# Six modulation rows copied to all partitions by DMA through DRAM, in place of GpSimd's partition broadcast, in a diffusion block with a 32-expert layer

## The chip, the cores and the metric

The kernel runs on one core of a Trainium2 chip. The metric is the device time of one execution in microseconds, as the median of several executions. Names of engines in the rows: PE is TensorE's matmul side (PEld its weight loads), DVE is VectorE, ACT is ScalarE, POOL is GpSimd, SP is SyncE, which here only issues DMAs. A name with a q (SPq, ACTq) is the engine's instruction queue.

## The reference

One layer over 256 latent tokens and 256 context tokens of width 1024, all in float32. What bears on the change:

```python
mod = (silu(c) @ w_mod + b_mod)[:, None, :]
sh1, sc1, g1, sh2, sc2, g2 = split(mod, 6)          # six rows of 1024 numbers, one for all tokens
u = modulate(rmsnorm(x, norm1_g), sh1, sc1)         # h * (1 + scale) + shift
p = u @ w_in
q, k, v, a_raw, beta = gdn_inputs(p, conv_w, rows)
o, _, _ = gdn_bidir(q, k, v, a_raw, beta, a_log, dt_bias, s_f, s_b)   # chunked scan, both directions
x = x + g1 * merge_branches(p, o, gdn_norm_g, w_fourier_out, w_gdn_out, w_merge_out)
h2 = modulate(rmsnorm(x, norm2_g), sh2, sc2)
x = x + g2 * moe_ffn(h2, ...)                       # top 4 of 32 experts, 3 matrices of 1024x1024 each
return rmsnorm(x, final_norm_g)
```

merge_branches gates two branches with sigmoid(p @ columns) and maps them to width 1024 three times (w_gdn_out, w_fourier_out, w_merge_out).

## The kernel before

Tokens lie on the 128 partitions in two tiles for the last stages. So the rows g1, sh2, (1 + sc2) * norm2_g and g2, which are the same for every token, are wanted as tiles of 128 equal rows. `fill_mod` computes them as two tiles `mr` (kept in `mrow2`) whose partitions 0, 32, 64 and 96 hold four pieces of 512 numbers: `mrow2[0]` holds g1 and sh2, `mrow2[1]` holds (1 + sc2) * norm2_g and g2. The helper `spread` then makes a 128 x 512 tile of one piece. Six calls stand in the text after the loop over w_gdn_out (tiles with the tags ff, ye and bv, which other stages used before), two more (g2b) at the start of the experts:

```python
def spread(b, j, dst):
    G.partition_broadcast(dst, mrow2[b][32 * j:32 * j + 1, :])
    return dst
```

Weights of the first part arrive in pieces of 128 x 1024 (`raw`, three buffers, issued by SP in a fixed order). `wsplit` makes two rounded halves of each: `hi` is a copy by ACT (line 156) and `lo = raw - hi` by POOL or DVE (line 157); three buffers of each. A product is three matmuls, lines 164 to 166 (w_hi by u_hi, w_hi by u_lo, w_lo by u_hi), so that the matmul of line 166 is the first that needs `lo`. SP can issue the piece after the next two only when `lo` of a piece is done.

A scheduler sets each engine's order when the program is built, and each engine then runs its list strictly in order. In the stretch of interest the scan over chunks (lines 725 to 787) is interleaved with matmuls that don't depend on it. The last of these are the eight gates b0 to b7 of `fill_gates` (`gate(1, j, ...)`, psum tile `ps_pf`, output `gb`): POOL makes `lo` for b0, b2, b4 and b6, DVE for the others. After the scan come its normalization (line 825 squares on ACT, 827 on DVE, 829 `ms` on POOL, 831 on DVE, transposes 837 on PE), the eight pieces of w_gdn_out, eight pieces of w_merge_out, the router, and the experts.

The experts' weights (384 transfers of 1 MB, `we`, line 809) are issued by SP, up to 17 ahead, each into a page that a matmul must first have released. At the start of the experts POOL makes `ow` (line 1075), the two g2b tiles, `g2r` (line 1179) from them, and `biasr` (lines 981 and 984), which the matmul of line 1112 needs.

Of the kernel before, what the change touches and what calls it, by code (L numbers as in the profile page):

```python
# [10 lines left out]
F32 = mybir.dt.float32  # L11
# [86 lines left out]
def hybrid_block(es: ExitStack, tc: tile.TileContext, cst, x, c, ctx, c_ctx, w_mod, b_mod, norm1_g, norm2_g, w_in,  # L98
# [3 lines left out]
    V, A, G, PE, SP = nc.vector, nc.scalar, nc.gpsimd, nc.tensor, nc.sync  # L102
# [13 lines left out]
    def P(tag):  # L116
        return ps.tile([128, 512], F32, name="ps_" + tag, tag=tag, bufs=_nb[tag])

    def T(tag):
        return tmp.tile([128, 512], F32, name=tag, tag=tag, bufs=_tb[tag])  # L120

    def sm(name, *shape):
        return cp.tile([128, *shape], F32, name=name)
# [7 lines left out]
    def load(src, name, tag="pg"):  # L131
        t_ = page(name, tag=tag)
        n = src.shape[1]
        SP.dma_start(out=t_.rearrange("p (a b) -> p a b", a=n), in_=src)
        return t_.rearrange("p (a b) -> p a b", a=n)
# [67 lines left out]
    for hc in range(2):  # L203
        wm.append([page("wm").rearrange("p (k w n) -> p k w n", k=2, w=2) for k in range(4)])
        for k in range(8):
            SP.dma_start(out=wm[hc][k // 2][:, k % 2],
                         in_=w_mod[0, k * 128:(k + 1) * 128, 0:2048].rearrange("p (w n) -> p w n", w=2)[:, :, 512 * hc:512 * hc + 512])
# [65 lines left out]


    mrow2 = []

    def fill_mod():
        for b in range(2):
            o = 2048 + 2048 * b
            mr = T("mr") if b == 0 else sm("mr1", 512)  # L280
            V.memset(mr, 0.0)
            G.dma_start(out=mr[0:128:32, :], in_=b_mod[0, o:o + 2048].rearrange("(j n) -> j n", j=4))
            pm = P("pf")
            for k in range(8):
                wq = load(w_mod[0, k * 128:(k + 1) * 128, o:o + 2048].rearrange("p (a n) -> p a n", a=4), "wmb")
                for j in range(4):
                    mm(pm[32 * j:32 * j + 32, :], scT[:, k, :], wq[:, j, :], start=(k == 0), stop=(k == 7))
                yield
            if b == 1:
                nr = T("rr")  # L290
                V.memset(nr, 1.0)
                G.dma_start(out=nr[0:64:32, :], in_=norm2_g.rearrange("o (j n) -> (o j) n", j=2))
                V.tensor_scalar_add(mr[0:64], mr[0:64], 1.0)
            V.tensor_tensor(out=mr, in0=pm, in1=mr, op=ALU.add)
            if b == 1:
                V.tensor_tensor(out=mr, in0=mr, in1=nr, op=ALU.mult)
            mrow2.append(mr)

    def take(gen, n=1):
        for _ in range(n):  # L300
            next(gen, 0)

    fm = fill_mod()
    pb = P("pf")
    for k in range(8):
# [16 lines left out]
        j = 32 * (k % 4)  # L322
# [134 lines left out]
    for t2 in range(2):  # L457
        pv = pkk[t2].rearrange("p (m n) -> p m n", n=64)
        kd = T("bv").rearrange("p (m n) -> p m n", n=64)
        q = slice(8 * t2, 8 * t2 + 8)  # L460
# [247 lines left out]
    for s in range(2):  # L708
# [3 lines left out]
        for n in range(4):  # L712
# [8 lines left out]
            for g in range(2):  # L721
                gs = slice(512 * g, 512 * g + 512)
                bv = T("bv")
# [22 lines left out]
                if not last:  # L746
                    ye = T("ye")
# [99 lines left out]
    for j in range(8):  # L847
# [7 lines left out]
        V.tensor_tensor(out=mg[:, 0:256], in0=mg[:, 0:256], in1=gab[0][:, j, :], op=ALU.add)  # L855
        A.copy(mT[0][:, j, :], mg[:, 0:256])
        V.tensor_tensor(out=mT[1][:, j, :], in0=mg[:, 0:256], in1=mT[0][:, j, :].bitcast(F32), op=ALU.subtract)
    def spread(b, j, dst):
        G.partition_broadcast(dst, mrow2[b][32 * j:32 * j + 1, :])
        return dst  # L860

    g1b, sh2b, a2b = [[spread(b, 2 * q + j, T(tag)) for j in range(2)] for b, q, tag in ((0, 0, "ff"), (0, 1, "ye"), (1, 0, "bv"))]
    x_pg = load(x[0].rearrange("(t p) d -> p t d", p=128), "x_pg", "pk")
    h2 = page("h2", tag="pk").rearrange("p (t d) -> p t d", t=2)

# [88 lines left out]
    tmp2 = es.enter_context(tc.tile_pool(name="tmp2", bufs=2, reuse_waits="tile"))  # L954
# [18 lines left out]
    def bias_parts():  # L973
        braw = T("xg", 2, 1024)
        for b, src in enumerate((b_gate, b_up)):
            for g in range(2):
                for part in range(2):
                    r = slice(64 * g + 32 * part, 64 * g + 32 * part + 32)
                    A.dma_start(out=braw[r, 512 * b:512 * b + 512], in_=src[0, :, 512 * g:512 * g + 512])
        A.dma_start(out=bdn[64:96, :], in_=b_down[0])  # L980
        G.tensor_copy(biasr, braw)
        for g in range(2):
            r = slice(64 * g + 32, 64 * g + 64)
            G.tensor_tensor(out=biasr[r], in0=braw[r], in1=biasr[r].bitcast(F32), op=ALU.subtract)
        iv = ident.rearrange("p (g l e) -> p g l e", g=2, l=2)
        V.tensor_tensor(out=pick.rearrange("p (g e) -> p g e", g=2), in0=iv[:, :, 0, :], in1=iv[:, :, 1, :], op=ALU.add)
        V.tensor_reduce(out=half, in_=pick.bitcast(F32).rearrange("p (g e) -> p g e", g=2), axis=AX.X, op=ALU.add)
# [75 lines left out]
    last_ow, last_xg = [None], [None]  # L1063
# [108 lines left out]
    cur, pend = pair(0), None  # L1172
    with tc.issue_after(last_xg[0]):
        bias_parts()
    with tc.issue_after(last_ow[0]):
        g2b = [spread(1, 2 + g, tmp2.tile([128, 512], F32, name="g2b", bufs=2)) for g in range(2)]
        g2r = tmp2.tile([128, 512], F32, name="g2r", bufs=1)
        for g in range(2):
            G.tensor_copy(g2r[64 * g:64 * g + 64], g2b[g][64 * g:64 * g + 64])
# [65 lines left out]
```

## Time and profile before

| what | value |
|---|---|
| median of three executions | 1444.76 us (1444.62 to 1446.91) |
| the profiled execution, its own time | 1448.83 us |
| its span, first to last instruction | 1446.9 us |
| PE, PEld busy share | 90%, 46% |
| DVE, ACT, POOL busy share | 35%, 17%, 19% |
| mean granted TensorE clock | 0.968 |
| moved by DMA | 469.74 MB, mean 325 GB/s |

Times in rows are of the profiled execution and count from the start of its span. A busy share is a mean over stages that differ; in the rows below each stage is taken by itself.

### The profile page before, as it was taken

The numbers are of one execution on the slowest core, as the hardware profiler recorded it, in microseconds if no ns is written. First come the engines' busy times: TensorE is split into PE (matmuls) and PEld (weight loads), VectorE is DVE, ScalarE is ACT, GpSimd is POOL, SyncE is SP. The second block draws the span as 40 slices with busy tenths as digits, with TensorE's granted clock in tenths as the row PEclk, the third lists the DMA queues.
The fourth block names the chain that finished last, engine by engine and source line by source line (L and its number), as shares of the span: only waits on it lengthen the run. The fifth ranks groups of instructions, "written<-read, shape, count | busy, mean of one in ns | idle before, by whom it ended". The sixth has DMA issues, their size and how long they took to land. (4 is left out here: it accounts for less than half of the span.)

```text
span 1446.9 us, 18887 instructions
## 1 busy us (share of the span) xinstructions
PE 1303.9 (90%) x7761; PEld 664.9 (46%) x7761; DVE 510.8 (35%) x965; ACT 243.7 (17%) x434; POOL 276.6 (19%) x256
## 2 busy tenths in 40 slices
PE   4997859899779889999999999999999999999996
PEld 2667858578569634333333333233333333333331
DVE  3579994655348411225112111211121112111213
ACT  3443333233224200000000000000000000000001
POOL 2434336544233130000100000001000000010000
PEclk9998979999879899999999999999999999999999
DMA  9962222124336999999999999999999999999994
GB/s 323 377 249 74 73 60 75 45 78 112 88 131 223 397 406 418 420 398 419 420 421 421 421 421 421 422 420 421 421 421 421 421 421 421 422 420 421 420 422 201
DMA packets 121159, 469.74 MB, mean 325 GB/s; under 512 B 10302, under 2 KB 63782, under 8 KB 69872
## 3 DMA queue, kind: packets, MB, share of 16 engines
q1 hardware_dynamic: 119696, 466.44, 81.0%
q10 hardware_dynamic: 1088, 1.89, 0.4%
q8 instruction: 62, 1.02, 0.3%
q0 software_dynamic: 288, 0.19, 0.2%
q14 instruction: 25, 0.20, 0.0%
HBM read 467.44 MB, written 1.05 MB: 324 GB/s over the span
## 5 line engine op out<-in xcount | busy, mean ns | idle before, releaser
L1111 PE MATMUL ps_gu<-we,xg 128*64 128x512 f32 x2048 | 469.6, 598 | 0.0
L1111 PEld LDWEIGHTS ps_gu<-we,xg 128*64 128x64 f32 x2048 | 141.2, 137 | 293.4 <-issue 280.2
L1134 PE MATMUL ps_dn<-we,aT 128*64 128x512 f32 x1024 | 237.3, 600 | 0.7 <-SPq L1146 0.4
L1100 POOL CAST rowsel<-pick 128x128 fp32r<-128x128 f32 x32 | 9.7, 304 | 684.5 <-PE ps_gu L1112 684.5
L157 POOL TENSOR_TENSOR lo<-raw,hi 128x1024 fp32r<-128x1024 f32 x44 | 106.3, 2418 | 157.6 <-ACT hi L156 123.2
L1143 DVE TENSOR_TENSOR x_pg<-x_pg,ps_st 128x512 f32<-128x512 f32 x128 | 82.6, 685 | 125.7 <-PE ps_st L1141 125.7
L1134 PEld LDWEIGHTS ps_dn<-we,aT 128*64 128x64 f32 x1024 | 66.9, 136 | 120.5 <-issue 113.7
L1117 ACT ACTIVATE sg<-gt 128x512 f32<-128x512 f32 x32 | 20.1, 629 | 448.1 <-DVE gt L1115 423.6
L1119 DVE TENSOR_SCALAR up<-ps_gu 128x512 f32<-128x512 f32 x32 | 22.1, 691 | 196.0 <-PE ps_gu L1112 189.2
L1137 DVE TENSOR_TENSOR ys<-ps_dn,g2r 128x512 f32<-128x512 f32 x32 | 22.1, 692 | 195.9 <-PE ps_dn L1134 195.9
L1141 PE MATMUL ps_st<-ys,wT 64*128 64x512 f32 x256 | 77.3, 641 | 12.8 <-DVE ys L1137 12.0
L156 ACT CAST hi<-raw 128x1024 fp32r<-128x1024 f32 x64 | 66.9, 1047 | 124.5 <-PE ps_pf L165 38.1
L164 PE MATMUL ps_pj<-u,hi 128*128 128x256 f32 x224 | 68.8, 310 | 18.1 <-DVE a L391 18.1
L1126 ACT COPY aT<-ps_tp 128x512 f32<-128x512 f32 x32 | 18.8, 586 | 322.0 <-PE ps_tp L1124 322.0
L1083 PEld LDWEIGHTS ps_tp<-oh,h 128*128 128x128 f32 x512 | 64.6, 201 | 14.1 <-issue 13.3
L391 DVE SCALAR_TENSOR_TENSOR a<-ps_pj,cvw,a 128x189 f32<-128x189 f32 (+3 forms) x152 | 63.8, 432 | 18.0 <-ACT a L388 16.3
L1083 PE MATMUL ps_tp<-oh,h 128*128 128x128 f32 x512 | 68.9, 290 | 1.1 <-DVE oh L1070 1.1
L1115 DVE TENSOR_SCALAR gt<-ps_gu 128x512 f32<-128x512 f32 x32 | 22.2, 692 | 133.2 <-issue 95.4
L165 PE MATMUL ps_pj<-u,hi 128*128 128x256 f32 x224 | 68.8, 308 | 0.0
L166 PE MATMUL ps_pj<-u,lo 128*128 128x256 f32 x224 | 67.2, 301 | 0.0
L1121 POOL TENSOR_TENSOR up<-up,sg 128x512 f32<-128x512 f32 x32 | 40.4, 1263 | 96.1 <-DVE up L1120 96.1
L164 PEld LDWEIGHTS ps_pj<-u,hi 128*128 128x128 f32 x224 | 46.0, 207 | 25.6 <-issue 23.8
(352 smaller groups left out, 1663.7 us busy)
## 6 DMA issues: line engine op xcount, KB each, us to landing
we<-in_w_gate_dram SPq DMA_DIRECT2D x128, 1024.0 KB, 18.4
we<-in_w_up_dram SPq DMA_DIRECT2D x128, 1024.0 KB, 17.8
we<-in_w_down_dram SPq DMA_DIRECT2D x128, 1024.0 KB, 18.9
raw<-in_w_in_dram SPq DMA_DIRECT2D x44, 512.0 KB, 4.0
wmb<-in_w_mod_dram SPq DMA_DIRECT2D x16, 1024.0 KB, 12.8
wm<-in_w_mod_dram SPq DMA_DIRECT2D x16, 512.0 KB, 8.1
raw<-in_w_gdn_out_dram SPq DMA_DIRECT2D x8, 512.0 KB, 4.1
raw<-in_w_merge_out_dram SPq DMA_DIRECT2D x8, 512.0 KB, 3.5
```

Of the source, the lines that this page charges most:

```text
L156: A.copy(hi, r)
L157: eng.tensor_tensor(out=lo, in0=r, in1=hi.bitcast(F32), op=ALU.subtract)
L164: mm(out_, sh_, mh_, start=start and i == 0, stop=False)
L165: mm(out_, sh_, ml_, start=False, stop=False)
L166: mm(out_, sl_, mh_, start=False, stop=stop and i == n - 1)
L391: V.scalar_tensor_tensor(out=ov, in0=iv, scalar=wap, in1=ov, op0=ALU.mult, op1=ALU.add)
L1083: mm(p[:, kl * n:(kl + 1) * n], h2[:, t, rows2(k)], oh[:, n * t:n * t + n], start=(t == 0), stop=(t == 1))
L1111: mm(p[64 * g:64 * g + 64, :], xg[:, k, :], w[:, 512 * g:512 * g + 512], start=(k == 0), stop=False)
L1121: G.tensor_tensor(out=up, in0=up, in1=sg, op=ALU.mult)
L1134: mm(p[64 * g:64 * g + 64, :], aT[:, f % 4, 64 * (f // 4):64 * (f // 4) + 64], w[:, 512 * g:512 * g + 512], start=(f == 0), stop=(f == 7))
L1141: mm(p, wT[64 * g:64 * g + 64, t * 128:(t + 1) * 128], ys[64 * g:64 * g + 64, :], start=True, stop=True)
L1143: V.tensor_tensor(out=x_pg[:, t, gsl], in0=x_pg[:, t, gsl], in1=p, op=ALU.add)
```

## The change

After `fill_mod` has made an `mr` tile, SP writes its four used partitions to a scratch array `mdram` in DRAM (2 x 4 x 512 numbers). Each `spread` becomes one DMA that reads 512 numbers of it once for each of the 128 partitions. The six of the tags ff, ye and bv are issued by SP, the two g2b by ACT. POOL no longer takes part in them. The g2b transfers are asked for after the last `xg` copy instead of after the last `ow`.

```diff
     mrow2 = []
+    dram = es.enter_context(tc.tile_pool(name="dram", bufs=1, space=bass.MemoryType.DRAM))
+    mdram = dram.tile([2, 4, 512], F32, name="mdram")
...
             mrow2.append(mr)
+            SP.dma_start(out=mdram[b], in_=mr[0:128:32, :])
...
-    def spread(b, j, dst):
-        G.partition_broadcast(dst, mrow2[b][32 * j:32 * j + 1, :])
+    def spread(b, j, dst, q):
+        q.dma_start(out=dst, in_=mdram[b, j:j + 1, :].broadcast_to([128, 512]))
         return dst
-    g1b, sh2b, a2b = [[spread(b, 2 * q + j, T(tag)) for j in range(2)] for b, q, tag in ((0, 0, "ff"), (0, 1, "ye"), (1, 0, "bv"))]
+    g1b, sh2b, a2b = [[spread(b, 2 * q + j, T(tag), SP) for j in range(2)] for b, q, tag in ((0, 0, "ff"), (0, 1, "ye"), (1, 0, "bv"))]
...
+    with tc.issue_after(last_xg[0]):
+        g2b = [spread(1, 2 + g, tmp2.tile([128, 512], F32, name="g2b", bufs=2), A) for g in range(2)]
     with tc.issue_after(last_ow[0]):
-        g2b = [spread(1, 2 + g, tmp2.tile([128, 512], F32, name="g2b", bufs=2)) for g in range(2)]
         g2r = tmp2.tile([128, 512], F32, name="g2r", bufs=1)
```

The scheduler makes new lists from this. Line numbers of the changed kernel are 3 to 4 higher from `fill_mod` on. The first place is POOL's list from the last gates to the normalization. In the kernel before, these rows follow the last `bv` products of the scan (L859 is `spread`; a row "ISA" without names is a change of the engine's configuration ahead of the instructions that follow; `lo` are the halves for gates b2, b4 and b6 and the first w_gdn_out piece):

```order
L157 ISA
L157 TENSOR_TENSOR lo<-raw,hi 128x1024
L859 ISA
L859 ISA ye<-mr 128x512
L859 ISA bv<-mr_531 128x512
L157 ISA
L157 TENSOR_TENSOR lo<-raw,hi 128x1024
L859 ISA
L859 ISA bv<-mr_531 128x512
L157 ISA
L157 TENSOR_TENSOR lo<-raw,hi 128x1024
L829 TENSOR_TENSOR ms<-ms,mh 128x8
```

In the changed kernel the same place of POOL's list reads:

```order
L728 TENSOR_TENSOR bv<-vtokx,mix 64x512 x2
L157 TENSOR_TENSOR lo<-raw,hi 128x1024 x3
L832 TENSOR_TENSOR ms<-ms,mh 128x8
L157 TENSOR_TENSOR lo<-raw,hi 128x1024
L832 TENSOR_TENSOR ms<-ms,mh 128x8
```

The broadcasts and the changes of configuration on both sides of them are gone, and the three `lo` stand next to each other ahead of `ms`; the order of what stays is the same.

The second place is SP's list in the same stretch (raw pieces of w_in are the gates' weights, x_pg a reload of the input). Before:

```order
L148 DMA raw<-in_w_in_dram 128x8x128 x5
L134 DMA x_pg<-in_x_dram 128x2x1024
L148 DMA raw<-in_w_in_dram 128x8x128 x3
L148 DMA raw<-in_w_gdn_out_dram 128x8x128 x6
L809 DMA we<-in_w_gate_dram 128x2048 x2
```

In the changed kernel:

```order
L148 DMA raw<-in_w_in_dram 128x8x128 x4
L862 DMA ye<-mdram 128x512
L148 DMA raw<-in_w_in_dram 128x8x128
L862 DMA ye<-mdram 128x512
L134 DMA x_pg<-in_x_dram 128x2x1024
L148 DMA raw<-in_w_in_dram 128x8x128
L862 DMA bv<-mdram 128x512
L148 DMA raw<-in_w_in_dram 128x8x128 x2
L862 DMA bv<-mdram 128x512
L148 DMA raw<-in_w_gdn_out_dram 128x8x128 x6
L812 DMA we<-in_w_gate_dram 128x2048 x2
```

Four of the new transfers now stand between the gates' pieces; each waits until its target tile is free. The two writes of `mdram` and the two ff transfers stand earlier in the same list, the second write between the third and the fourth piece of w_in that follow the last `wmb` loads.

The third place is POOL's list at the start of the experts. Before:

```order
L1075 TENSOR_TENSOR ow<-oh,wt 128x4x64 x2
L859 ISA
L859 ISA g2b<-mr_531 128x512 x2
L1075 ISA
L1075 TENSOR_TENSOR ow<-oh,wt 128x4x64 x2
L1179 COPY g2r<-g2b 64x512 x2
L981 CAST biasr<-xg 128x1024
L984 TENSOR_TENSOR biasr<-xg,biasr 32x1024 x2
```

In the changed kernel:

```order
L1078 TENSOR_TENSOR ow<-oh,wt 128x4x64 x4
L984 CAST biasr<-xg 128x1024
L1183 COPY g2r<-g2b 64x512
L987 TENSOR_TENSOR biasr<-xg,biasr 32x1024 x2
L1183 COPY g2r<-g2b 64x512
```

The first `g2r` copy, which now waits for a DMA, stands ahead of the subtraction that completes `biasr`.

## Rows read from the trace of the kernel before

**Rows 1.** Stages: length, busy PE, PEld, DVE, ACT, POOL; clock, DMA share, GB/s.
```profile
281.00:371.00 90.00, 89.66 (x786) 72.87 (x786) 49.34 (x139) 28.36 (x42) 38.14 (x26) 1.00 0.32 89
371.00:424.00 53.00, 32.17 (x237) 27.02 (x235) 18.98 (x42) 17.12 (x55) 18.41 (x10) 0.83 0.32 87
424.00:468.00 44.00, 42.26 (x301) 41.80 (x302) 29.53 (x38) 15.26 (x24) 12.15 (x5) 0.86 0.61 213
468.00:500.00 32.00, 25.45 (x189) 24.42 (x189) 17.30 (x39) 9.27 (x22) 5.44 (x6) 0.84 1.02 421
500.00:512.00 12.00, 12.00 (x58) 4.72 (x56) 0.72 (x3) 1.64 (x2) 1.48 (x2) 1.00 0.94 304
512.00:1420.00 908.00, 863.03 (x3972) 316.27 (x3968) 187.88 (x292) 64.66 (x111) 74.52 (x97) 1.00 1.01 420
```

**Rows 2.** Timeline of PE around three waits: start, duration, instruction, [idle before <-releaser].
```profile
372.76 0.39 PE L166 MATMUL ps_pf<-u,lo 128*128 128x256 f32 x1 [1.50 <-POOL lo L157]
...
373.78 1.09 PE L773 MATMUL ps_sc<-a,qk 64*64 64x128 f32 x16
...
391.80 0.58 PE L166 MATMUL ps_pf<-u,lo 128*128 128x256 f32 x1 [8.78 <-POOL lo L157]
...
394.23 1.69 PE L773 MATMUL ps_sc<-a,qk 64*64 64x128 f32 x16
...
409.38 0.58 PE L166 MATMUL ps_pf<-u,lo 128*128 128x256 f32 x1 [7.78 <-POOL lo L157]
...
413.64 1.35 PE L837 MATMUL ps_sc<-cs,o 128*128 128x128 f32 x5
```

**Rows 3.** Two short stretches of the same view as rows 1.
```profile
392.00:396.00 4.00, 4.00 (x28) 3.60 (x30) 0.02 (x1) 0.02 (x1) 0.00 (x0) 0.56 0.78 201
...
409.00:412.50 3.50, 3.12 (x14) 3.12 (x15) 1.48 (x1) 0.00 (x0) 3.50 (x3) 0.50 0.50 148
```

**Rows 4.** Timeline of POOL, 370 to 411 us.
```profile
370.34 2.36 POOL L157 TENSOR_TENSOR lo<-raw,hi 128x1024 fp32r<-128x1024 f32 x1 [6.62 <-issue]
380.20 1.47 POOL L859 PARTITION_BROADCAST ye<-mr  x1 [7.50 <-ACT gb L621]
...
389.42 2.33 POOL L157 TENSOR_TENSOR lo<-raw,hi 128x1024 fp32r<-128x1024 f32 x1 [7.08 <-issue]
399.29 0.80 POOL L859 PARTITION_BROADCAST bv<-mr  x1 [7.54 <-PE ps_pf L166]
407.00 2.33 POOL L157 TENSOR_TENSOR lo<-raw,hi 128x1024 fp32r<-128x1024 f32 x1 [6.90 <-issue]
409.30 1.68 POOL L829 TENSOR_TENSOR ms<-ms,mh 128x8 f32<-128x8 f32 x1
```

**Rows 5.** Timeline of DVE, ACT and SP, single rows.
```profile
120.82 0.72 DVE L296 TENSOR_TENSOR mr<-mr,rr 128x512 f32<-128x512 f32 x1
...
136.33 1.04 ACT L156 CAST hi<-raw 128x1024 fp32r<-128x1024 f32 x1 [2.37 <-issue]
...
372.73 19.41 SPq L148 DMA_DIRECT2D raw<-in_w_in_dram  x3
...
376.98 1.12 DVE L738 SCALAR_TENSOR_TENSOR rr<-ps_sc,mix,bv 128x128 f32<-128x128 f32 x4
...
383.20 1.04 ACT L156 CAST hi<-raw 128x1024 fp32r<-128x1024 f32 x1
```

**Rows 6.** Timeline of ACT's queue, POOL and PE at the start of the experts.
```profile
504.54 0.43 ACTq L980 DMA_DIRECT2D ov<-in_b_down_dram  x1
...
516.90 1.19 POOL L1075 TENSOR_TENSOR ow<-oh,wt 128x256 f32<-128x256 f32 x2 [11.41 <-issue]
...
525.27 1.22 PE L1112 MATMUL ps_gu<-biasr,rowsel 128*128 128x512 f32 x2 [4.73 <-POOL biasr L984]
```

**Rows 7.** DMA issues by line: KB each, median us from issue to landing.
```profile
we<-in_w_down_dram SPq DMA_DIRECT2D x128, 1024.0 KB, 18.9
...
fng<-in_final_norm_g_dram ACTq DMA_DIRECT2D x1, 512.0 KB, 7.9
```

## The prediction

> **What bounds the kernel now.** I first cut the span into stages by what DMA and PE do in them [rows 1]. From 512 to 1420 us the DMA engines are busy all the time (share 1.01) and move 420 GB/s. PE is busy for 863 of those 908 us, so it has some slack. This long stretch is the stream of expert weights: it takes as long as its bytes take, and nothing that the change removes makes it shorter. The stream is already at its full rate from 468 us on, while before 468 the DMA engines are busy for a third to two thirds of the time. So the end comes earlier by as much as the stage before 468 ends earlier. That is the place to look.
>
> In that part I looked for times in which PE, which executes its list strictly in order, does nothing. From 281 to 371 it is busy for 89.66 of 90 us at clock 1.00 [rows 1]: whatever POOL does there, PE has other work, and a faster POOL gives nothing. From 371 to 424 PE is busy for only 32 of 53 us. The timeline of PE shows why [rows 2]: three waits, each ended by a `lo` of POOL, at the first matmul that needs the low half of gates b2, b4 and b6: 1.50, 8.78 and 7.78 us, together 18.1 us.
>
> Why those halves are late stands in POOL's timeline [rows 4]. The halves themselves take 2.36, 2.33 and 2.33 us, the broadcasts between them 0.80 us each. But each time POOL goes from broadcasts to other work or back, it is idle for 6.62 to 7.54 us. Some of these idle times carry the name of another engine (gb, ps_pf), others "issue", yet their lengths are nearly the same in both directions, and the order of the lists puts a change of configuration at each. I read all five as the price of that change. The half for b6 shows the size: its input `hi` is ready at 383.20 + 1.04 = 384.2 [rows 5], and it starts at 407.00, after two changes each way.
>
> **The change, part by part.** *Removed in the scan stage.* POOL keeps the three halves and `ms`, with nothing between. Is then a wait left? The latest is that for b6. PE reached it at 409.38 - 7.78 = 401.6. Without the first two waits, and with the clock's part that is worked out below, it comes there at 401.6 - 1.5 - 8.8 - 1.7 = 389.6. `lo` would be done by 384.2 + 2.4 = 386.6, or earlier, since ACT's copies move forward too. So all three waits go: 18.1 us. As a check, the first `ms` follows the half for b6: it ran at 409.30 [rows 4], and could run at about 387, 22 us earlier, so the normalization behind it doesn't hold PE where POOL held it.
>
> *The clock.* After the two long waits the granted clock is down: 0.56 in the stretch from 392 and 0.50 from 409 [rows 3], that is 1.2 GHz in place of 2.4 for most of the first and all of the second. After the short wait PE does 8 matmuls in 373.78 - 372.76 = 1.02 us, 0.128 us each. After the second it does 10 in 394.23 - 391.80 = 2.43 us, 1.15 more than at that rate, and the 16 small ones of line 773 take 1.69 in place of 1.09 us. After the third it does 22 in 413.64 - 409.38 = 4.26 us, 1.45 more [rows 2]. Together 3.2 us, which go with the idle times that PE had before them. The first part ends 18.1 + 3.2 = 21.3 us earlier.
>
> The stretch from 424 to 468 has a clock of 0.86 [rows 1]. If PE arrived there at full clock and kept it, the same work would take 0.86 x 44 = 37.8 us, 6.2 less. I count 0, because short waits of the normalization, which stay, lie ahead of it; 6.2 is the other end.
>
> *Removed at the experts.* POOL's `ow` waits 11.41 us for a change of configuration, `biasr` is late by that, and PE waits 4.73 us for it [rows 6]. I count this at nothing: the weights flow at 420 GB/s meanwhile, and PE's slack makes up for it. From 500 to 512 DMA does 304 GB/s; if a quicker start closed that gap, it would give 12 x (1 - 304/420) = 3.3 us, an upper end.
>
> *Added.* Two writes of 8 KB and eight copies of 128 x 2 KB = 0.262 MB. Six copies, 1.57 MB, lie in stretches with a DMA share of 0.32: hidden, and 3.7 us at 420 GB/s if that cover were gone. The two g2b copies lie in the stream: 0.524 MB at 420 GB/s are 1.25 us. They start near the gap from 500 to 512 and could be free; I take 1.25, since the stream is full right after.
>
> A rule of the Trainium skill (DMA: Bandwidth & Descriptors, section "Issuing engines are not separate DMA queues") speaks against the change here: transfers asked for by ACT run on the same 16 engines and interleave with SP's. By it the 1.25 us count, as I count them; if ACT had engines of its own, the sum would be 21.3. No row here shows which.
>
> *SP's list.* The second write of `mdram` holds SP until DVE has made `mr`, at 120.82 + 0.72 = 121.5. The piece behind it, landing within the 7.9 us that another 512 KB transfer took [rows 7], is there by 130; ACT takes it up at 136.33 [rows 5]. No cost. The last `bv` copy waits until the scan has read its tile, at 376.98 + 1.12 = 378.1, or earlier with PE's first wait gone. Behind it wait the pieces of w_gdn_out. Ahead of it are the gates' last three, which SP issued from 372.73 over 19.41 us, since each needs a `lo` to free its buffer [rows 5]; the halves now come earlier. I count no cost.
>
> *The order at the experts.* `biasr` now waits for the first `g2r` copy and so for a g2b transfer. That is issued right behind the row at 504.54, at about 505.5. `biasr` was ready at 525.27 [rows 6], with about 5.5 us of POOL's work behind the copy. A landing within 14 us makes nothing later. The nearest row, a copy of one row to all partitions issued by ACT in the middle of the stream, is 7.9 us [rows 7]; the longest is 18.9, which would make PE wait 5 us longer than before.
>
> **Sum.** 18.1 + 3.2 - 1.25 = 20.0 us. The profiled execution, 1448.83 us, would become 1428.8. It is 4.1 us above the median of the runs, so against the median: 1444.76 - 20.0 = **1424.8 us**.
>
> The Trainium skill (GPSIMD Engine Reference, section "2.1 Instruction dispatch") gives about 6 us for the load of code at the first call after such a change. The five idle times here come to 35.6 us [rows 4], against an estimate of 29.8 from that figure, and that at the experts is 11.41. By the figure of the page POOL would be 5.8 us less late and the sum about 14, an estimate; the sum above goes by the rows.
>
> **Rivals.** *SP's waits take POOL's place.* SP is held at a `ye` or `bv` copy, a gate's piece comes late, and one of the two long waits of PE comes back from another cause with its slow clock. For it: SP's list is strict, and four of the new transfers stand between these pieces. Against it: the tiles are free by 378.1, and PE needs the last gates on the new time axis only near 390. Gain 20.0 - 8.8 - 1.7 = 9.5 us: 1435.3.
>
> *Hidden anyway.* The first part ends earlier, but the experts don't start earlier, so that the stream only fills its 17 pages sooner and then stands still, as it half does from 500 to 512 already. Against it: the router and the first expert hang on the same chain of PE, DVE and ACT as the last raw pieces. About 1444.8.
>
> *Slower: a late g2b.* If 128 reads of one row of DRAM in a full stream are slow, POOL stands at `g2r`, PE at the matmul of line 1112, no page is released, and the stream stops. From a landing of 14 us on, each further us costs up to one; the gain is gone at 14 + 20 = 34 us, and the kernel is slower by over 0.2% from 37 us. At 45 us it would take 1444.8 + 11 = 1456. The longest landing in rows 7 is half of what decides.
>
> **How the numbers follow.** A measurement of this kernel can tell about 0.2%, 2.9 us. The forecast has a chance of 0.75: its own range is from 1416 (a full clock from 424 on, or the gap closed, on top of the sum) to 1430 (g2b costs PE its 5 us). SP's waits have 0.12, hidden 0.06, slower 0.05, and 0.02 is left for a larger gain. The range reaches from 1416 to 1436 and takes in the first rival. Faster by over 0.2%: 0.88; within it: 0.06; slower: 0.06.
>
> **What would show it.** In the profile of the changed kernel POOL should do the halves for b2, b4 and b6 each right behind its `hi`, PE should have no wait for `lo` from 371 to the transposes of line 837 (new line 840), and these should start near 392 in place of 413.64. DMA should be at its full rate from about 447. The g2b copies should land within 14 us, and the matmul of line 1112 wait for nothing or less than before. The prediction is wrong if PE's idle time between 371 and 424 returns under the name of a raw transfer or of ACT's `hi`, or if the stream's full stretch is longer than before by more than 1.25 us.

## The result and the profile after

The changed kernel takes **1422.69 us** (median of 4 executions, 1421.02 to 1423.22), the kernel before in the same comparison 1444.69 us (1443.41 to 1446.91). The ratio is 0.9844, 95% interval 0.9827 to 0.9861: 22.0 us less, where 20.0 were forecast.

The windows of the changed kernel, with the columns of [rows 1]. All their edges but the first are those of [rows 1] less 21.3 us, the forecast for the first part, so they don't cut the work at quite the same places (the counts of matmuls stand behind PE's time). The last is the full stretch of the stream.

```profile
281.00:371.00 90.00, 90.00 (x792) 72.38 (x791) 47.91 (x136) 29.63 (x43) 37.29 (x23) 1.00 0.41 115
371.00:402.70 31.70, 28.77 (x219) 26.04 (x218) 18.49 (x39) 15.65 (x53) 11.79 (x5) 0.88 0.61 191
402.70:446.70 44.00, 43.46 (x354) 42.88 (x354) 34.55 (x40) 19.22 (x32) 15.29 (x6) 0.97 0.67 230
446.70:478.70 32.00, 25.87 (x156) 18.84 (x156) 11.15 (x34) 5.63 (x14) 4.09 (x7) 0.84 1.02 402
...
490.70:1398.70 908.00, 862.42 (x3950) 313.83 (x3952) 189.75 (x295) 64.66 (x111) 67.24 (x92) 1.00 1.01 420
```

PE's 21 idle us between 371 and 424 have shrunk to 2.9. DMA is at its full share in the window from 446.7 us, as it was in the one from 468, and the full stretch has the rate that it had, 420 GB/s. Then follows all that PE waited for in the changed kernel from 281 to 405 us (engine, operation and line, what ended the wait, sum, times, longest):

```profile
PE ps_sc L840 <- DVE o L834: 2.6, 2, 2.0
PE ps_sc L876 <- DVE sh2c L873: 0.3, 1, 0.3
```

No wait for a `lo` is left in that stretch; the normalization's two short ones are, and one of 0.3 us at the router. POOL's timeline in the same stretch answers to [rows 4]:

```profile
356.14 2.35 POOL L157 TENSOR_TENSOR lo<-raw,hi 128x1024 fp32r<-128x1024 f32 x1 [3.51 <-ACT hi L156]
367.43 2.36 POOL L157 TENSOR_TENSOR lo<-raw,hi 128x1024 fp32r<-128x1024 f32 x1 [8.93 <-ACT hi L156]
377.89 2.36 POOL L157 TENSOR_TENSOR lo<-raw,hi 128x1024 fp32r<-128x1024 f32 x1 [8.10 <-ACT hi L156]
380.36 1.64 POOL L832 TENSOR_TENSOR ms<-ms,mh 128x8 f32<-128x8 f32 x1
```

POOL still stands idle ahead of the halves, for 3.51 to 8.93 us, but now these times end with ACT's `hi`: POOL waits for its input, and nobody waits for POOL. PE reaches the first transposes of the normalization at 386.90, where [rows 2] had 413.64:

```profile
367.39 1.09 PE L776 MATMUL ps_sc<-a,qk 64*64 64x128 f32 x16
...
377.72 1.09 PE L776 MATMUL ps_sc<-a,qk 64*64 64x128 f32 x16
...
386.90 0.71 PE L840 MATMUL ps_sc<-cs,o 128*128 128x128 f32 x5
...
394.16 1.52 PE L840 MATMUL ps_sc<-cs,o 128*128 128x128 f32 x5 [2.02 <-DVE o L834]
```

The two rows of line 776 (773 before) are the scan's pieces that [rows 2] shows at 373.78 and 394.23. From the first of them to the transposes PE took 413.64 - 373.78 = 39.86 us; now it takes 386.90 - 367.39 = 19.51 us.

**One execution against another.** The span fell by 1446.9 - 1420.4 = 26.5 us, more than the median. The profiled execution of before was 4.1 us above its median, and already at line 773 it was 6.4 us behind the changed one, of which only 1.5 are its first wait. I therefore profiled both kernels again and read the gain between marks inside one execution; the last four rows are kernels of the experiments below. The marks are starts in the timelines: line 773 or 776 (second of the three scan pieces there), the first transposes, SP's last w_merge_out piece, ACT's first square of the final norm.

| run | scan piece | to transposes | to last raw piece | to final norm | span |
|---|---|---|---|---|---|
| before | 373.78 | 39.86 | 52.24 | 972.1 | 1446.9 |
| before_again | 373.32 | 39.50 | 49.37 | 970.1 | 1441.3 |
| change | 367.39 | 19.51 | 49.32 | 975.3 | 1420.4 |
| change_again | 369.46 | 19.51 | 48.34 | 973.0 | 1419.2 |
| change_third | 372.30 | 19.51 | 49.25 | 972.1 | 1422.0 |
| g2b_only | 369.71 | 40.39 | 48.46 | 972.6 | 1440.2 |
| scan_copies_only | 372.44 | 19.51 | 49.27 | 971.5 | 1421.6 |
| ff_on_pool | 367.75 | 19.51 | 49.18 | 972.0 | 1417.4 |
| grouped_on_pool | 370.16 | 19.51 | 50.31 | 971.1 | 1420.0 |

So the gain has one place: the second column, 39.50 to 40.39 us with broadcasts between the halves and 19.51 without. The first wait (1.50 us in before, 1.98 in before_again) lies ahead of it, in the first column, where executions scatter by up to 5 us. The third column shows no gain beyond its scatter: 48.46 to 52.24 with the waits, 48.34 to 50.31 without. In the fourth the four profiles in which POOL makes g2b took 970.1 to 972.1 us and the five in which a DMA does 972.0 to 975.3, 1.8 us more on the mean.

### The profile page after: what moved, and what is told of

Read it like the earlier page. It is cut to its first block, busy times and chain, and to the rows that moved or that the text cites. A ratio compares the mean times of both kernels' runs of the same rounds, so it can differ in the third digit from the quotient of the medians.

```text
span 1420.4 us, 18877 instructions
## 1 busy us (share of the span) xinstructions
PE 1298.9 (91%) x7761; PEld 656.9 (46%) x7761; DVE 507.6 (36%) x965; ACT 243.4 (17%) x434; POOL 270.5 (19%) x248
## 5 line engine op out<-in xcount | busy, mean ns | idle before, releaser
L1144 PE MATMUL ps_st<-ys,wT 64*128 64x512 f32 x256 | 77.1, 649 | 12.8 <-DVE ys L1140 12.0
L164 PE MATMUL ps_pj<-u,hi 128*128 128x256 f32 x224 | 68.1, 307 | 18.3 <-DVE a L394 18.3
```

The source lines that it names most:

```text
L164: mm(out_, sh_, mh_, start=start and i == 0, stop=False)
L1144: mm(p, wT[64 * g:64 * g + 64, t * 128:(t + 1) * 128], ys[64 * g:64 * g + 64, :], start=True, stop=True)
```

## The experiments

**change_again, before_again and change_third** are the changed kernel, the kernel before, and the changed kernel once more.

> The changed kernel once more, on the same chip as the parts: 1422.7 us within 1. All theories expect the same; it is what the parts are compared with.

> The kernel before, unchanged, for a second profile. Its first profile holds one DVE instruction of line 657 (62 elements, 2.37 us from 199.16) next to a POOL half that started at 199.11; in the profile of the changed kernel the same instruction took 0.21 us, and that part ran 4.65 us ahead from there on. Theory (chance of which of the two started first, no effect of the change): the second profile may show either, and without it the span is near 1442 us. Rival (the change itself moved that part): the instruction takes about 2.4 us again and the span is near 1447.

> The changed kernel once more, as the base of the two kernels with extra transfers in this call: 1422 to 1426 us.

Measured: change_again 1425.23 us (1421.01 to 1427.51, 4 executions) against 1446.12 for before beside it, ratio 0.9865 (0.9847 to 0.9884); that is 2.5 us above the value that was expected within 1. before_again, one execution, 1443.29, with a span of 1441.3: the instruction of line 657 took 2.37 us again, and yet the span was the shorter one, so neither of the two expected pairs came. change_third 1423.8 (1420.12 to 1425.82, 5) against 1447.14, ratio 0.9835 (0.9812 to 0.9858). The gain is 20.9 to 23.3 us in three comparisons, and before_again's waits for `lo` are the same three, 16.7 us.

**scan_copies_only** undoes the part at the experts: the six rows by DMA, the two g2b by POOL.

> The six copies of the scan stage go by DMA, the two g2b tiles are again made by POOL's broadcast. Theory (the whole gain is POOL's halves for gates b2, b4, b6; the change of configuration at the experts is hidden under the weights): the gain of the full change and the 1.25 us of g2b bytes on top, 1421.5 us, at most 1 us either way. Rival (the late biasr at the experts holds pages and so the stream): 3 to 5 us slower than the full change, 1426 to 1428.

```diff
+    def spread_pool(b, j, dst):
+        G.partition_broadcast(dst, mrow2[b][32 * j:32 * j + 1, :])
+        return dst
...
-    with tc.issue_after(last_xg[0]):
-        g2b = [spread(1, 2 + g, tmp2.tile([128, 512], F32, name="g2b", bufs=2), A) for g in range(2)]
     with tc.issue_after(last_ow[0]):
+        g2b = [spread_pool(1, 2 + g, tmp2.tile([128, 512], F32, name="g2b", bufs=2)) for g in range(2)]
```

**g2b_only** is its counterpart: the six rows by POOL, g2b by DMA.

> The six copies of the scan stage stay POOL broadcasts, only the two g2b tiles go by DMA. Theory: no gain, 1444.7 + 1.25 = 1446 us, within 1.5. Rival (the experts' start is worth something): 1440 to 1442 us.

```diff
...
-    g1b, sh2b, a2b = [[spread(b, 2 * q + j, T(tag), SP) for j in range(2)] for b, q, tag in ((0, 0, "ff"), (0, 1, "ye"), (1, 0, "bv"))]
+    g1b, sh2b, a2b = [[spread_pool(b, 2 * q + j, T(tag)) for j in range(2)] for b, q, tag in ((0, 0, "ff"), (0, 1, "ye"), (1, 0, "bv"))]
```

Measured: scan_copies_only 1423.33 us (1422.42 to 1424.03, 5 executions), ratio 0.9847 (0.9832 to 0.9862), 0.8 above what was expected at most but not above the change beside it (1425.23); g2b_only 1444.73 us (1437.53 to 1450.88, 12), ratio 0.9987 (0.997 to 1.0004). The six copies are the whole gain that can be told from the scatter. What PE waited for in g2b_only, 281 to 430 us:

```profile
PE ps_pf L166 <- POOL lo L157: 18.3, 3, 8.7
PE ps_sc L840 <- DVE o L834: 2.5, 2, 2.1
```

The three waits are there, and from the scan piece to the transposes it takes 40.39 us; scan_copies_only takes 19.51. At the experts of scan_copies_only POOL still pays for both changes of configuration, in a stream that is already full:

```profile
468.46 1.30 POOL L1082 TENSOR_TENSOR ow<-oh,wt 128x256 f32<-128x256 f32 x2 [6.68 <-DVE oh L1077]
478.57 1.48 POOL L862 PARTITION_BROADCAST g2b<-mr  x2 [8.81 <-issue]
487.69 1.19 POOL L1082 TENSOR_TENSOR ow<-oh,wt 128x256 f32<-128x256 f32 x2 [7.64 <-issue]
```

That costs 8.81 + 7.64 us of POOL and nothing of the kernel: the time is that of the change. Here PE had no wait for `biasr`. PE's 4.73 us of [rows 6] are one execution's: in before_again the same wait was 2.14 us, behind a change of configuration of 8.89 us in place of 11.41.

**ff_on_pool** puts one pair of broadcasts back, at a place where PE never waits.

> Like the full change, but the two ff tiles are made by POOL, with the two changes of configuration of about 5.5 and 7 us that they bring near 295 to 309 us, where PE is busy without a gap. Theory (only what stands between the last gates' halves counts): the same as the full change, 1422.7, within 1.5 us. Rival (every change of configuration costs its time): 1422.7 + 5 to 14 = 1428 to 1437 us.

```diff
...
-    g1b, sh2b, a2b = [[spread(b, 2 * q + j, T(tag), SP) for j in range(2)] for b, q, tag in ((0, 0, "ff"), (0, 1, "ye"), (1, 0, "bv"))]
+    g1b = [spread_pool(0, j, T("ff")) for j in range(2)]
+    sh2b, a2b = [[spread(b, 2 * q + j, T(tag), SP) for j in range(2)] for b, q, tag in ((0, 1, "ye"), (1, 0, "bv"))]
```

Measured: 1422.58 us (1419.13 to 1424.35, 5 executions), ratio 0.9844 (0.9829 to 0.986). POOL's timeline has the two idle times:

```profile
296.62 1.48 POOL L862 PARTITION_BROADCAST ff<-mr  x2 [5.80 <-ACT zT L527]
305.11 3.01 POOL L728 TENSOR_TENSOR bv<-vtokx,mix 64x512 f32<-64x512 f32 x2 [7.01 <-PE ps_pf L166]
```

12.8 us of POOL, and PE busy for 90.00 of the 90 us from 281 to 371. A change of configuration costs what waits for it, here nothing.

**grouped_on_pool** has no copy by DMA at all: it is the kernel before, with its six broadcasts in one group behind the half of the third w_gdn_out piece.

> The kernel before, with one thing moved: POOL makes all six tiles of the scan stage in one group, asked for after its half of the third w_gdn_out piece, so that one pair of changes of configuration stays, behind the gates' halves and ms. Theory (the number and the place of the changes cost, not the broadcast): the three waits of PE go as in the full change; the group takes 6.5 + 4.8 + 7 = 18.3 us in an idle stretch of POOL of 15.7 us, so the next half is about 2.6 us late: 1444.7 - 21.3 + 2.6 = 1426 us, between 1423 and 1428. Rival (the gain needs the broadcasts off POOL): 1435 us or more.

```diff
...
+        if j == 2:
+            after_lo = last_lo[-1]
...
-    g1b, sh2b, a2b = [[spread(b, 2 * q + j, T(tag)) for j in range(2)] for b, q, tag in ((0, 0, "ff"), (0, 1, "ye"), (1, 0, "bv"))]
+    with tc.issue_after(after_lo):
+        g1b, sh2b, a2b = [[spread(b, 2 * q + j, T(tag)) for j in range(2)] for b, q, tag in ((0, 0, "ff"), (0, 1, "ye"), (1, 0, "bv"))]
```

Measured: 1426.52 us (1420.43 to 1428.67, 6 executions) against 1445.53, ratio 0.9865 (0.9834 to 0.9897). POOL's timeline:

```profile
403.41 1.48 POOL L862 PARTITION_BROADCAST ff<-mr  x2 [6.68 <-issue]
404.75 1.46 POOL L862 PARTITION_BROADCAST ye<-mr  x2
406.07 1.46 POOL L862 PARTITION_BROADCAST bv<-mr  x2
414.47 2.40 POOL L158 TENSOR_TENSOR lo<-raw,hi 128x1024 fp32r<-128x1024 f32 x1 [6.94 <-DVE a L857]
```

Six broadcasts take 4.4 us and two changes 13.6, and from the scan piece to the transposes it takes 19.51 us as in the changed kernel. PE waited 0.9 us for `lo` in the whole stretch to 470. So the broadcast as such was never what cost: it was its place between the halves.

**extra_copies_in_stream** multiplies the suspected cost of the g2b transfers: 32 further copies of that kind, whose data nothing reads.

> The changed kernel with 32 more copies of one row to 128 partitions, one for each expert, asked for by ACT into a tile that nobody reads any more: 32 x 0.262 = 8.4 MB more in the stretch of the weights. Theory (that stretch takes as long as its bytes): 8.4 MB at 420 GB/s are 20.0 us more, 1442.7 us, within 2. Rival (PE sets the pace there, or transfers of another engine's queue are free): within 3 us of 1422.7.

```diff
...
+        with tc.issue_after(last_at[0]):
+            A.dma_start(out=mrow2[1], in_=mdram[1, 2:3, :].broadcast_to([128, 512]))
         if el == 0:
             wT = cur[1]()
```

Measured: 1453.14 us (1450.11 to 1454.84, 12 executions), ratio to before 1.0051 (1.0031 to 1.007): 28 to 30 us over the changed kernel, not 20. The run mixes three things. Its timeline shows the last copies behind the weights, on ACT's queue ahead of the output's:

```profile
1415.12 14.28 ACTq L1193 DMA_DIRECT2D mr<-mdram  x4
...
1437.02 0.33 ACTq L1193 DMA_DIRECT2D mr<-mdram  x1
...
1440.10 0.33 ACTq L1193 DMA_DIRECT2D mr<-mdram  x1
1440.47 0.46 ACTq L1222 DMA_DIRECT2D out_dram<-x_pg  x1
1443.90 0.33 ACTq L1193 DMA_DIRECT2D mr<-mdram  x1
1444.27 0.47 ACTq L1222 DMA_DIRECT2D out_dram<-x_pg  x1
1447.09 0.33 ACTq L1193 DMA_DIRECT2D mr<-mdram  x1
```

All go to one tile, so each waits for the one before it. Only 24 were issued by 1388 us, while weights still flowed, and the last four lengthen the tail: from the final norm to the end it took 15.0 us in place of 8.9. And ACT's other work stood behind them, which PE's waits from 490 to 1400 us show (the `xg` of line 1087):

```profile
PE ps_tp L1129 <- POOL up L1126: 28.6, 26, 1.5
PE ps_gu L1116 <- ACT xg L1087: 19.3, 5, 6.2
```

The DMA engines kept their rate all the same, with ACT's copies in it:

```profile
490.00:1388.00 898.00, 837.40 (x3826) 306.16 (x3824) 182.45 (x284) 62.13 (x108) 72.04 (x94) 0.98 1.01 420
```

So PE's waits for `xg` didn't stop the stream up to there. The bytes of 32 copies are 20.0 us; of the 8 to 10 us above that, 6.1 are the tail, and where the rest comes from isn't shown. The price of a byte couldn't be read from this run's time. It took two cleaner ones.

**row_copies_on_sp and plain_copies_on_sp**: 24 extra transfers in SP's list instead, one behind every third matrix, so that ACT and the tail are untouched. The first reads one row 128 times, the second 128 different rows.

> The changed kernel with 24 further copies of one row to 128 partitions (256 KB each, 6.29 MB) that only cost transfer time: SP issues each behind the first transfer of one matrix in three, into a tile that nothing reads any more, so that neither ACT's list nor the end of the kernel is touched. In extra_copies_in_stream the copies stood in ACT's list and eight of them came after the last weights; from the end of the first part to the final norm it took about 21 us longer for the 24 that lay in the stream, 0.87 us each. Theory 'the stream pays for bytes': 6.29 MB at 420 GB/s are 15.0 us, so the time is that of the changed kernel in this call plus 15 us, and the rest of the 28 us before came from ACT's list and from the tail. Rival 'a row copied to 128 partitions costs more than its bytes': plus 21 us, with a full stretch of the stream whose GB/s is lower than 420.

> The same 24 transfers at the same places, with 128 different rows of 512 numbers of the input as their source in place of one row that is read 128 times. Theory 'bytes': the same 15 us more than the changed kernel, within 2 us of row_copies_on_sp. Rival 'reading one row 128 times is what costs': about 15 us here and 21 us there.

```diff
-            SP.dma_start(out=t_, in_=w[0, e, 256 * i:256 * i + 256, :].rearrange("(p r) n -> p r n", r=2))
+            ld = SP.dma_start(out=t_, in_=w[0, e, 256 * i:256 * i + 256, :].rearrange("(p r) n -> p r n", r=2)).ins
             ahead.append(t_)
+            if i == 0 and 7 <= m < 79 and m % 3 == 1:
+                with tc.issue_after(ld):
+                    SP.dma_start(out=mrow2[1], in_=mdram[1, 2:3, :].broadcast_to([128, 512]))
```

In plain_copies_on_sp the source is `x[0][0:128, 0:512]`. Measured: 1439.23 us (1437.68 to 1442.97, 6 executions) and 1439.68 us (1437.26 to 1442.43, 6), with change_third at 1423.8 beside them: 15.4 and 15.9 us more, where the bytes give 15.0. The full stretch of row_copies_on_sp:

```profile
490.70:1398.70 908.00, 856.28 (x3916) 308.79 (x3912) 186.40 (x290) 63.39 (x109) 66.98 (x91) 1.00 1.01 420
```

The rate is 420 GB/s as ever; PE does 3916 matmuls in it, where the changed kernel did 3950. The rival, a row that costs more than its bytes, is refuted: 0.64 us a copy, and the plain rows cost the same.

## Why the prediction was right

*Where the bound is, and three waits of 18.1 us.* Right. g2b_only keeps the three waits and the time; every kernel without broadcasts between the last halves takes 19.51 us from the scan piece to the transposes. The three waits were 16.7 us in before_again and 18.3 in g2b_only.

*The clock, 3.2 us.* Right in kind, too low in size. From the scan piece to the transposes PE does the same work, within a matmul, in the kernel before and in the changed one, which does it at full clock without a gap (columns of [rows 1]):

```profile
373.78:413.64 39.86, 23.30 (x184) 20.52 (x184) 10.03 (x19) 10.70 (x41) 11.62 (x7) 0.79 0.28 75
...
367.39:386.90 19.51, 19.51 (x185) 17.38 (x184) 10.84 (x26) 10.73 (x42) 7.92 (x4) 1.00 0.47 128
```

PE's busy time fell by 3.8 us; against before_again (24.64 us) and g2b_only (23.97) it is 5.1 and 4.5. Whether all of that is the clock isn't shown. With all three waits it makes 21.9, 21.9 and 22.8 us; less 1.25 for g2b's bytes, 20.6 to 21.5. That is 0.6 to 1.5 us above the forecast 20.0; the rest of the measured 20.9 to 23.3 lies within the scatter of the comparisons.

*The stretch from 424 to 468, counted at 0 with 6.2 as the other end.* Right, as far as the runs tell. The window from 402.7 above has a clock of 0.97, but it starts later in the work than that from 424 did. Cut 44 us long from 10.4 us behind the first transposes, as that one lies, it looks like this in before_again, g2b_only and the change:

```profile
423.20:467.20 44.00, 43.48 (x329) 42.91 (x330) 31.00 (x38) 17.61 (x29) 14.70 (x6) 0.90 0.67 229
...
420.50:464.50 44.00, 43.27 (x341) 42.85 (x340) 32.28 (x39) 17.66 (x29) 14.71 (x6) 0.93 0.68 234
...
397.26:441.26 44.00, 43.46 (x332) 42.88 (x332) 31.61 (x39) 17.56 (x29) 14.74 (x6) 0.91 0.65 223
```

The first two keep the long waits ahead of it and the third doesn't, and they do the same there. The 0.86 of [rows 1] belongs to that execution. The short waits hold the clock down, as I expected, but not for long. Two windows of the changed kernel, and one of before:

```profile
396.00:404.00 8.00, 7.74 (x37) 7.34 (x36) 1.90 (x7) 0.96 (x4) 0.00 (x0) 0.50 0.78 305
406.00:412.00 6.00, 6.00 (x53) 6.00 (x52) 5.21 (x7) 3.28 (x5) 2.40 (x1) 1.00 0.33 90
...
424.00:432.00 8.00, 7.87 (x37) 7.87 (x38) 1.26 (x5) 0.10 (x1) 0.00 (x0) 0.50 0.69 278
```

After the 2.02 us wait that ends at 394.16, ahead of the last transposes, PE runs at the lower level, 1.2 GHz, and from 406 it is back at 2.4 GHz. In before the same stretch stood at the lower level too.

*The experts' late start, counted at 0.* Right: g2b_only is within its noise of before, and scan_copies_only of the change, though PE's wait in the changed kernel, 1.19 us, is shorter than in both profiles of before (4.73 and 2.14):

```profile
490.92 0.96 PE L1115 MATMUL ps_gu<-biasr,rowsel 128*128 128x512 f32 x3 [1.19 <-POOL biasr L987]
```

*g2b's bytes, 1.25 us.* The price is right: 0.64 us a copy is 1.3 for two. On the time of the change it can't be seen, since scan_copies_only and the three medians of the change lie within 2.5 us of one another. From the last raw piece on the profiles with g2b by DMA took 1.8 us longer on the mean, which agrees, but the two groups touch (970.1 to 972.1, 972.0 to 975.3). The sign set for this, a full stretch longer by more than 1.25 us, was finer than that scatter and decides nothing. The Trainium skill (DMA: Bandwidth & Descriptors, section "Issuing engines are not separate DMA queues") has transfers of all engines share the same 16 engines; the extra copies bear it out from both queues, since the engines together moved 420 GB/s with ACT's copies and with SP's, and no more than without.

*SP's waits, and the landing of g2b.* Both harmless, as counted. The transfers' rows of the changed kernel (KB each, median us to landing):

```profile
ye<-mdram SPq DMA_DIRECT2D x2, 256.0 KB, 5.1
...
g2b<-mdram ACTq DMA_DIRECT2D x2, 256.0 KB, 8.8
```

The limit was 14 us, the nearest row 7.9 us. The last `bv` copy was issued at 371.73, ahead of the estimate of 378.1.

*The rivals.* SP in POOL's place and a stream that hides the gain are out by the table of marks: the 20 us of the second column arrive at the end almost whole. The late g2b is out by its landing.

*The mark at 392.* The transposes started at 386.90. That is 5 us better than forecast, by luck: the profiled execution of before was as far behind before the change could act. Against before_again and change_third, whose scan pieces lie 1 us apart, the mark moves from 412.82 to 391.81.

*The idle time at a change of configuration.* The Trainium skill (GPSIMD Engine Reference, section "2.1 Instruction dispatch") has about 6 us; by it the sum would have been about 14, an estimate. The idle times shown here stand at 5.80 to 11.41 us, and the gain bears out the rows. The 14 didn't follow from the page, though: the sum adds up PE's waits, which were measured whatever a single change costs.

## What to carry to other kernels

Look at the order of an engine's list before its busy share: POOL was 19% busy, and four broadcasts of 0.8 us held PE for 18 us because they stood at three places between pieces of other work, with a change of configuration on both sides of each place. The other two of the six stood where PE didn't wait. Move such an operation out of a chain, group it where nobody waits, or give it to a DMA; here grouping alone, with no DMA, brings a ratio of 0.9865 where the DMAs bring 0.9835 to 0.9865, with intervals that overlap. Price an added transfer in a saturated stream by its bytes at the stream's rate, and look separately at what stands behind it in the list of the engine that issues it.

## What the runs showed of the hardware

*A DVE instruction is held by a half of POOL, or not, by 0.1 us of chance.* In the profiled execution of before, and in the changed one, at the same point of the program:

```profile
199.11 2.34 POOL L157 TENSOR_TENSOR lo<-raw,hi 128x1024 fp32r<-128x1024 f32 x1 [1.38 <-ACT hi L156]
199.16 2.37 DVE L657 TENSOR_TENSOR tt<-tt,prod 128x62 f32<-128x62 f32 x1
```

```profile
198.93 2.43 POOL L157 TENSOR_TENSOR lo<-raw,hi 128x1024 fp32r<-128x1024 f32 x1 [1.43 <-ACT hi L156]
198.93 0.21 DVE L660 TENSOR_TENSOR tt<-tt,prod 128x62 f32<-128x62 f32 x1
```

Sixty-two elements on each partition take 0.21 us, or 2.37. It was 2.34 to 2.38 in before, before_again, change_again, change_third, scan_copies_only and row_copies_on_sp, where POOL's half starts 0.04 to 0.09 us before it. It was 0.20 or 0.21 in the change, g2b_only, ff_on_pool, grouped_on_pool, extra_copies_in_stream and plain_copies_on_sp, where POOL starts at most 0.03 us before it or 0.01 after. So it is not an effect of the change. On the mean the scan piece starts 2.3 us later in the first six, though the two groups overlap: part of the scatter ahead of the change, and a reason to compare two traces from a mark behind such places.

*A change of configuration costs POOL idle time, in both directions.* It is 5.80 to 8.81 us in the rows above, with the longer ones in the full stream, where [rows 6] had 11.41. One broadcast between two subtractions thus costs about 15 us of POOL for 0.8 us of work.
